# LayerNorm of x + residual: two loads moved ahead of the opening barrier, closing barriers dropped, wider x loads in a ring of 80 rows with a residual ring of 16

## Chip, cores, metric

One core of one Trainium2 chip. The metric is the device time of one execution in microseconds (us), of the slowest core (here the only one). "Span" is the time from the first to the last instruction that the profile records; the device time is 1.3 to 2.2 us longer, and that difference will matter. All timed runs that are compared here are fast, with a granted clock of 1.0.

The engines are named as in the profile: SP (SyncE) issues the large transfers, POOL (GpSimd), ACT (ScalarE) and DVE (VectorE) compute, PE (TensorE) does almost nothing here. SBUF and PSUM are the two memories on the chip.

## The reference

```python
# x, residual: (16, 1024, 512) float32; gamma, beta: (512,)
z = x + residual
mean = np.mean(z, axis=-1, keepdims=True)
var = np.var(z, axis=-1, keepdims=True)
return gamma * (z - mean) / np.sqrt(var + eps) + beta
```

That is 16384 rows of 512 numbers. The kernel puts 128 rows side by side in the 128 partitions, so it works on 128 "rows" per partition, and below a row always means one of these 128. One row of one tensor is 256 KB. x and residual are read and the result is written once: 100.7 MB in all.

## The kernel before

SP issues all large transfers on one queue, in program order. x is loaded into `zbuf` (a ring of 64 rows), residual into `rbuf` (a ring of 32). POOL adds residual to `zbuf`. ACT makes the mean and the sum of squares of each row. DVE normalizes in place, and SP stores from `zbuf`.

```python
X_CHUNKS = [8] * 15 + [4, 4]          # rows per load: 2 MB each, the last two 1 MB
R_CHUNKS = [8] * 15 + [4, 4]
OUT_CHUNKS = [16] * 7 + [8, 4, 4]     # 4 MB stores, the last three smaller
Z_ROWS = 64; R_ROWS = 32; STORE_LAG = 40; TURN = 8; JUNK = 4
...
    for c, (lo, n) in enumerate(loads_x):          # SP, in this order
        asked = lo + n
        while stored < asked - Z_ROWS:             # room in zbuf: an old store has landed
            ...; nc.sync.wait_ge(so[o], 16); ...
        nc.sync.dma_start(out=part(zbuf, Z_ROWS, lo, n), in_=dram(xf, lo, n)).then_inc(sx[c], 16)
        while todo_r and todo_r[0][1][0] + todo_r[0][1][1] <= asked:
            rc, (rlo, rn) = todo_r.pop(0)
            wait_rows(s_add, "add", rlo + rn - R_ROWS)   # room in rbuf: POOL has added
            nc.sync.dma_start(out=part(rbuf, R_ROWS, rlo, rn), ...).then_inc(sr[rc], 16)
        while todo_o and (olo + on <= asked - STORE_LAG or asked == total):  # (shortened)
            wait_rows(s_out, "out", olo + on)
            nc.sync.dma_start(out=dram(of, olo, on), in_=part(zbuf, ...)).then_inc(so[oc], 16)
...
    # ACT, in turns of 8 rows: every activation waits for the one 4 before it
    act.wait_ge(s_add, r0 + TURN)
    for k in range(2 * TURN):        # 8 Identity (mean), then 8 Square (variance)
        ...
        i.then_inc(s_act, 1).wait_op(s_act, due, "sem-ge")
    act.activation(out=std[...], in_=ssq[...], func=ACT.Sqrt, ...)
...
    # at the end: SP waits for the last stores, clears the semaphores;
    # leaving the tile context then adds drains and barriers of all engines
```

SP waits in order, so a wait of one transfer also holds back all later ones. And the load of residual rows that end at row r waits until POOL has added all rows up to r - R_ROWS.

Of the kernel before, what the change touches and what calls it, by code (L numbers as in the profile page):

```python
# [6 lines left out]

FP32 = mybir.dt.float32
ACT = mybir.ActivationFunctionType
ALU = mybir.AluOpType  # L10


X_CHUNKS = [8] * 15 + [4, 4]
R_CHUNKS = [8] * 15 + [4, 4]
OUT_CHUNKS = [16] * 7 + [8, 4, 4]

Z_ROWS = 64
R_ROWS = 32
STORE_LAG = 40


TURN = 8


JUNK = 4


@with_exitstack
def kernel(
# [9 lines left out]
    nc = tc.nc  # L39
    P = nc.NUM_PARTITIONS  # L40
    xf = x.flatten_outer_dims()
    rf = residual.flatten_outer_dims()
    of = out.flatten_outer_dims()
    N, D = xf.shape
    inv_d = 1.0 / float(D)
    total = N // P
    turns = total // TURN

    def spans(sizes):
        assert sum(sizes) == total  # L50
        return [(sum(sizes[:c]), n) for c, n in enumerate(sizes)]

    blocks = spans(OUT_CHUNKS)

    def dram(t, lo, n):

        b0, bn = next(b for b in blocks if b[0] <= lo and lo + n <= b[0] + b[1])
        v = t[P * b0 : P * (b0 + bn), :].rearrange("(p j) d -> p j d", p=P)
        return v[:, lo - b0 : lo - b0 + n, :].rearrange("p a b -> p (a b)")

    ctx.enter_context(tc.tile_critical())  # L61

    zbuf = nc.alloc_sbuf_tensor("zbuf", [P, Z_ROWS * D], FP32)
    rbuf = nc.alloc_sbuf_tensor("rbuf", [P, R_ROWS * D], FP32)
    gb_row = nc.alloc_sbuf_tensor("gb_row", [1, 2 * D], FP32)
# [3 lines left out]
    nm = nc.alloc_sbuf_tensor("nm", [P, total], FP32)  # L69
    ssq = nc.alloc_sbuf_tensor("ssq", [P, total], FP32)  # L70
# [1 line left out]
    rstd = nc.alloc_sbuf_tensor("rstd", [P, total], FP32)  # L72
    gamma_p = nc.alloc_psum_tensor("gamma_p", [P, D], FP32)
    beta_p = nc.alloc_psum_tensor("beta_p", [P, D], FP32)
    junk = [nc.alloc_psum_tensor(f"junk{i}", [P, D], FP32) for i in range(JUNK)]

    sems = []

    def sem(name):
        s = nc.alloc_semaphore(name)  # L80
        sems.append(s)
        return s

    loads_x, loads_r, stores = spans(X_CHUNKS), spans(R_CHUNKS), spans(OUT_CHUNKS)
    sx = [sem(f"sx{c}") for c in range(len(loads_x))]
    sr = [sem(f"sr{c}") for c in range(len(loads_r))]
    so = [sem(f"so{c}") for c in range(len(stores))]
    s_gb = [sem(f"gb{k}") for k in range(2)]
    s_const = sem("const")
    s_pe = sem("pe")  # L90
    s_add = sem("add")
    s_act = sem("act")
    s_std = sem("std")
    s_dve = sem("dve")
    s_out = sem("out")

    def part(buf, size, lo, n):
        assert lo % size + n <= size
        return buf[:, (lo % size) * D : (lo % size + n) * D]


    nc.scalar.dma_start(out=gb_row[:, :D], in_=gamma[None, :]).then_inc(s_gb[0], 16)
    nc.scalar.dma_start(out=gb_row[:, D:], in_=beta[None, :]).then_inc(s_gb[1], 16)
    nc.vector.memset(ones[:, :], 1.0).then_inc(s_const, 1)  # L104
    nc.vector.memset(eps_t[:, :], float(eps)).then_inc(s_const, 1)  # L105
    nc.tensor.wait_ge(s_const, 1)
# [6 lines left out]

    todo_r, todo_o = list(enumerate(loads_r)), list(enumerate(stores))
    seen = {"add": 0, "out": 0}

    def wait_rows(s, key, rows):
        if rows > seen[key]:
            nc.sync.wait_ge(s, rows)
            seen[key] = rows  # L120

    stored = 0
    for c, (lo, n) in enumerate(loads_x):
        asked = lo + n
        while stored < asked - Z_ROWS:
            o = next(i for i, b in enumerate(stores) if b[0] == stored)
            assert all(o != t[0] for t in todo_o)
            nc.sync.wait_ge(so[o], 16)
            stored += stores[o][1]
        nc.sync.dma_start(  # L130
            out=part(zbuf, Z_ROWS, lo, n), in_=dram(xf, lo, n)
        ).then_inc(sx[c], 16)
        while todo_r and todo_r[0][1][0] + todo_r[0][1][1] <= asked:
            rc, (rlo, rn) = todo_r.pop(0)
            wait_rows(s_add, "add", rlo + rn - R_ROWS)
            nc.sync.dma_start(  # L136
                out=part(rbuf, R_ROWS, rlo, rn), in_=dram(rf, rlo, rn)
            ).then_inc(sr[rc], 16)
        while todo_o and (
            todo_o[0][1][0] + todo_o[0][1][1] <= asked - STORE_LAG or asked == total  # L140
        ):
            oc, (olo, on) = todo_o.pop(0)
            wait_rows(s_out, "out", olo + on)
            nc.sync.dma_start(  # L144
                out=dram(of, olo, on), in_=part(zbuf, Z_ROWS, olo, on)
            ).then_inc(so[oc], 16)


    have_x = have_r = 0
    lo = 0  # L150
    while lo < total:
        n = min(loads_x[have_x][1], loads_r[have_r][1])
        nc.gpsimd.wait_ge(sx[have_x], 16)
        nc.gpsimd.wait_ge(sr[have_r], 16)
        assert loads_x[have_x] == loads_r[have_r] == (lo, n)
        z = part(zbuf, Z_ROWS, lo, n)
        nc.gpsimd.tensor_tensor(  # L157
            out=z, in0=z, in1=part(rbuf, R_ROWS, lo, n), op=ALU.add
        ).then_inc(s_add, n)
        have_x, have_r, lo = have_x + 1, have_r + 1, lo + n  # L160

    def row_at(zoff, k):
        return zbuf[:, bass.ds(zoff + k * D, D)]


    act = nc.scalar
    act.preload_act_table_set("sqrt_and_others")  # L167
    act.wait_ge(s_const, 2)
    act.sem_inc(s_act, JUNK)
    with act.Fori(0, turns) as t:  # L170
        zoff = act.snap((t * (TURN * D)) % (Z_ROWS * D))
        r0 = act.snap(t * TURN)

        n0 = act.snap(t * (2 * TURN))
        act.wait_ge(s_add, r0 + TURN)
        for k in range(2 * TURN):
            row = k % TURN


            due = act.lower_val(n0 + (k + 1))  # L180
            if k < TURN:
                i = act.activation(  # L182
                    out=junk[k % JUNK][:, :],
                    in_=row_at(zoff, row),
                    func=ACT.Identity,
                    scale=-inv_d,
                    accum_out=nm[:, bass.ds(r0 + row, 1)],
                )
            else:
                i = act.activation(  # L190
                    out=junk[k % JUNK][:, :],
                    in_=row_at(zoff, row),
                    func=ACT.Square,
                    bias=nm[:, bass.ds(r0 + row, 1)],
                    accum_out=ssq[:, bass.ds(r0 + row, 1)],
                )
            i.then_inc(s_act, 1).wait_op(s_act, due, "sem-ge")
        due = act.lower_val(n0 + (JUNK + 2 * TURN))
        act.activation(  # L199
            out=std[:, bass.ds(r0, TURN)],  # L200
            in_=ssq[:, bass.ds(r0, TURN)],
            func=ACT.Sqrt,
            bias=eps_t[:, 0:1],
            scale=inv_d,
        ).then_inc(s_std, TURN).wait_op(s_act, due, "sem-ge")


    dve = nc.vector
    dve.wait_ge(s_pe, 2)
    with dve.Fori(0, turns) as t:  # L210
        zoff = dve.snap((t * (TURN * D)) % (Z_ROWS * D))
        r0 = dve.snap(t * TURN)
        n0 = dve.snap(t * (2 * TURN))
        for k in range(TURN):
            due = dve.lower_val(n0 + (JUNK + TURN + k + 1))
            dve.scalar_tensor_tensor(  # L216
                out=row_at(zoff, k),
                in0=row_at(zoff, k),
                scalar=nm[:, bass.ds(r0 + k, 1)],
                in1=gamma_p[:, :],  # L220
                op0=ALU.add,
                op1=ALU.mult,
            ).wait_op(s_act, due, "sem-ge")
        due = dve.lower_val(r0 + TURN)
        dve.reciprocal(  # L225
            out=rstd[:, bass.ds(r0, TURN)], in_=std[:, bass.ds(r0, TURN)]
        ).then_inc(s_dve, TURN).wait_op(s_std, due, "sem-ge")
        for k in range(TURN):
            i = dve.scalar_tensor_tensor(  # L229
                out=row_at(zoff, k),  # L230
                in0=row_at(zoff, k),
                scalar=rstd[:, bass.ds(r0 + k, 1)],
                in1=beta_p[:, :],
                op0=ALU.mult,
                op1=ALU.add,
            )
            i.then_inc(s_out, 1)
            if k == 0:
                i.wait_op(s_dve, due, "sem-ge")


    for o, (lo, n) in enumerate(stores):
        if lo >= stored:
            nc.sync.wait_ge(so[o], 16)
    nums = sorted(s.num for s in sems)
    assert nums == list(range(nums[0], nums[-1] + 1)), nums
    nc.sync.sem_clear(range(nums[0], nums[-1] + 1))


# [33 lines left out]
```

## Time and profile before

| | before |
|---|---|
| time, median of 4 runs | 242.61 us (242.29 to 242.68) |
| span of the profiled run; its time | 240.0 us; 242.21 us |
| first load issued; first load landed | 0.94; 8.32 us |
| last store issued; landed | 231.14; 238.75 us |
| last landing to end of span | 1.28 us |

The landings are in the trace's semaphore records, which no view shown here prints: each transfer has 16 landing times there, one for each DMA engine, and a landing without further words is the last of them. The profile page says at once what the limit is; the digits are busy tenths in 40 slices of the span, 9 is 90% or more.

```profile
span 240.0 us, 1853 instructions
...
PE 4.1 (2%) x4; PEld 1.0 (0%) x4; DVE 178.7 (74%) x274; ACT 176.6 (74%) x529; POOL 142.2 (59%) x21
...
DVE  0000399999999999999997399944999359995950
ACT  2002999999999999999972999449993599959500
...
DMA  7999999999999999999999999999999999999994
GB/s 252 434 420 429 431 435 431 429 415 431 434 440 437 415 420 431 475 437 390 429 434 434 420 426 434 429 453 426 415 423 431 456 399 423 445 426 431 431 418 205
...
q1 hardware_dynamic: 6336, 100.67, 98.4%
```

DMA is at 9 in all slices but the first and last, at about 430 GB/s, and the queue's packets fill 98.4% of 16 engines' time. The Trainium skill ("DMA: Bandwidth & Descriptors", § Where 436 GB/s comes from) gives 435.2 GB/s as the ceiling of the SBUF ports; the trace agrees to 1%. ACT and DVE are at 9 in 26 of the 40 slices, yet they cost nothing while DMA is full.

SP's own timeline (start, duration, line, what) shows the opening: the first load goes out at 0.94 us, and eight more before any wait; the residual ring of 32 rows lets four residual loads go out at once.

```profile
0.94 0.39 SPq L130 DMA_DIRECT2D zbuf<-in_x_dram  x1
...
4.94 0.49 SPq L130 DMA_DIRECT2D zbuf<-in_x_dram  x1
22.17 0.33 SPq L136 DMA_DIRECT2D rbuf<-in_residual_dram  x1
```

How long that queue is can be read from the residual loads that went out between 40 and 90 us: the last line is the time from issue to landing.

```profile
L136 SPq DMA_DIRECT2D rbuf<-in_residual_dram x4: 328/379/431, 41.8 to 83.8; - x4
...
DMA to landing us min/median/max: 19.1/33.8/39.8
```

A residual load lands at least 19 us after its issue, although 2 MB take only 4.9 us to move. At least 14 us of other transfers stood before it. I call that time the lead.

The end, from the last store (issued at 231.1, landing 7.6 us later) and the barriers that follow:

```profile
L144 SPq DMA_DIRECT2D out_dram<-zbuf x1: 333/333/333, 231.1 to 231.1; - x1
...
DMA to landing us min/median/max: 7.6/7.6/7.6
```

```profile
L278 SPq EVENT_SEMAPHORE  x2: 17/17/17, 239.5 to 240.0; - x2
```

All five engines pass barriers until 240.0, after a last landing at 238.75.

The end of one of ACT's turns in the timeline:

```profile
32.28 0.67 ACT L190 ACTIVATE junk<-zbuf,nm 128x512 f32 x1
...
33.19 0.30 ACT L199 ACTIVATE std<-ssq,eps_t  x1
33.84 0.60 ACT L182 ACTIVATE junk<-zbuf 128x512 f32 x1 [0.35 <-issue]
```

The last Square starts at 32.28, the square root at 33.19 and the next turn at 33.84. A turn of 8 rows takes 11.41 us.

### The profile page before, as it was taken

Reading aid. Unit: us, or ns where it says so; the run is one execution under the profiler, and the core shown is the slowest. Engines: PE = TensorE matmul, PEld = TensorE weight load, DVE = VectorE, ACT = ScalarE, POOL = GpSimd, SP = SyncE. Lnnn points to the kernel's source line nnn. Section 1 sums busy time; section 2 is a strip of 40 time slices with the busy share of each in tenths; the row PEclk is TensorE's granted clock in tenths of the full one; section 3 lists DMA queues with packets and bytes.
Section 4 is the critical chain, followed back from the end, with each engine's and each line's share of the span. In section 5 each row is a group of like instructions: output and inputs, shape, how many; then the busy total and the mean of one; then the engine's idle time right before and its main releaser. Section 6 shows DMA issues by size and latency. Waiting matters only on the chain.

```text
span 240.0 us, 1853 instructions
## 1 busy us (share of the span) xinstructions
PE 4.1 (2%) x4; PEld 1.0 (0%) x4; DVE 178.7 (74%) x274; ACT 176.6 (74%) x529; POOL 142.2 (59%) x21
## 2 busy tenths in 40 slices
PE   3300000000000000000000000000000000000000
PEld 0000000000000000000000000000000000000000
DVE  0000399999999999999997399944999359995950
ACT  2002999999999999999972999449993599959500
POOL 0078989889899506894088920989109890860000
DMA  7999999999999999999999999999999999999994
GB/s 252 434 420 429 431 435 431 429 415 431 434 440 437 415 420 431 475 437 390 429 434 434 420 426 434 429 453 426 415 423 431 456 399 423 445 426 431 431 418 205
DMA packets 6341, 100.68 MB, mean 419 GB/s; under 512 B 706, under 2 KB 706, under 8 KB 708
## 3 DMA queue, kind: packets, MB, share of 16 engines
q1 hardware_dynamic: 6336, 100.67, 98.4%
q14 instruction: 1, 0.01, 0.0%
q10 hardware_dynamic: 4, 0.00, 0.0%
HBM read 67.11 MB, written 33.55 MB: 419 GB/s over the span
## 4 chain that ended last, share of the span: by engine, by line
DMA 56%; ACT 14%; issue 14%; POOL 6%; DVE 3%; SPq 2%; ACTq 2%; DVEq 0%; POOLq 0%
DMA out_dram<-zbuf 36%; DMA rbuf<-in_residual_dram 20%; ACT junk L190 9%; POOL zbuf L157 6%; ACT junk L182 5%; DVE zbuf L229 3%; SPq L130 1%; ACTq L180 1%; ACTq L182 1%; SPq L136 1%; ACT std L199 0%; SPq L144 0%; DVE rstd L225 0%; DVEq L229 0%; ACTq L170 0%
## 5 line engine op out<-in xcount | busy, mean ns | idle before, releaser
L157 POOL TENSOR_TENSOR zbuf<-zbuf,rbuf 128x4096 f32<-128x4096 f32 (+1 forms) x17 | 142.0, 8351 | 71.5 <-DMA rbuf<-in_residual_dram 71.5
L216 DVE SCALAR_TENSOR_TENSOR zbuf<-zbuf,nm,gamma_p 128x512 f32 x128 | 91.0, 747 | 50.8 <-ACT junk L190 50.8
L182 ACT ACTIVATE junk<-zbuf 128x512 f32 x128 | 74.4, 581 | 45.3 <-POOL zbuf L157 41.6
L229 DVE SCALAR_TENSOR_TENSOR zbuf<-zbuf,rstd,beta_p 128x512 f32 x128 | 85.7, 743 | 0.6
L190 ACT ACTIVATE junk<-zbuf,nm 128x512 f32 x128 | 86.1, 673 | 0.0
L190 ACT ACTIVATION_READ_ACCUMULATOR junk<-zbuf,nm x128 | 24.2, 189 | 0.0
L182 ACT ACTIVATION_READ_ACCUMULATOR junk<-zbuf x128 | 23.9, 187 | 0.0
L199 ACT ACTIVATE std<-ssq,eps_t x16 | 4.8, 301 | 1.6
L225 DVE RECIPROCAL rstd<-std x16 | 3.1, 196 | 0.0
L167 ACT ACT_TABLE_LOAD x1 | 1.3, 1283 | 1.7 <-SPq L61 1.7
L109 PE MATMUL beta_p<-gb_row,ones 1*128 1x512 f32 x2 | 2.1, 1136 | 2.4 <-DMA gb_row<-in_beta_dram 2.4
L109 PE MATMUL gamma_p<-gb_row,ones 1*128 1x512 f32 x2 | 2.0, 1122 | 2.3 <-DMA gb_row<-in_gamma_dram 2.3
L104 DVE MEMSET ones<- 1x128 f32 x1 | 0.2, 165 | 1.0 <-SPq L61 1.0
L109 PEld LDWEIGHTS beta_p<-gb_row,ones 1*128 1x128 f32 x2 | 0.5, 304 | 4.0 <-DMA gb_row<-in_beta_dram 4.0
L109 PEld LDWEIGHTS gamma_p<-gb_row,ones 1*128 1x128 f32 x2 | 0.5, 305 | 2.3 <-issue 2.3
L264 POOL MEMSET const-float32-0.0<- 128x1 f32 x1 | 0.1, 99 | 0.2 <-issue 0.2
L264 POOL MEMSET const-bfloat16-1.0<- 128x1 bf16 x1 | 0.1, 102 | 0.0
L264 POOL MEMSET const-uint8-127<- 128x1 uint8 x1 | 0.1, 102 | 0.0
L264 POOL MEMSET const-float32-1.0<- 128x1 f32 x1 | 0.1, 99 | 0.0
L105 DVE MEMSET eps_t<- 128x1 f32 x1 | 0.1, 59 | 0.0
## 6 DMA issues: line engine op xcount, KB each, us to landing
zbuf<-in_x_dram SPq DMA_DIRECT2D x15, 2048.0 KB, 32.8
rbuf<-in_residual_dram SPq DMA_DIRECT2D x15, 2048.0 KB, 30.4
out_dram<-zbuf SPq DMA_DIRECT2D x7, 4096.0 KB, 28.5
zbuf<-in_x_dram SPq DMA_DIRECT2D x2, 1024.0 KB, 32.6
rbuf<-in_residual_dram SPq DMA_DIRECT2D x2, 1024.0 KB, 34.6
out_dram<-zbuf SPq DMA_DIRECT2D x1, 2048.0 KB, 16.5
out_dram<-zbuf SPq DMA_DIRECT2D x2, 1024.0 KB, 7.7
gb_row<-in_gamma_dram ACTq DMA_DIRECT2D x1, 2.0 KB
```

The lines of the kernel that those rows point to most:

```text
L109: nc.tensor.matmul(dest[:, :], ones[:, :], gb_row[:, k * D : (k + 1) * D], start=True, stop=True).then_inc(s_pe, 1)
L130: nc.sync.dma_start(out=part(zbuf, Z_ROWS, lo, n), in_=dram(xf, lo, n)).then_inc(sx[c], 16)
L136: nc.sync.dma_start(out=part(rbuf, R_ROWS, rlo, rn), in_=dram(rf, rlo, rn)).then_inc(sr[rc], 16)
L157: nc.gpsimd.tensor_tensor(out=z, in0=z, in1=part(rbuf, R_ROWS, lo, n), op=ALU.add).then_inc(s_add, n)
L167: act.preload_act_table_set("sqrt_and_others")
L180: due = act.lower_val(n0 + (k + 1))
L182: i = act.activation(out=junk[k % JUNK][:, :], in_=row_at(zoff, row), func=ACT.Identity, scale=-inv_d, accum_out=nm[:, bass.ds(r0 + row, 1)],)
L190: i = act.activation(out=junk[k % JUNK][:, :], in_=row_at(zoff, row), func=ACT.Square, bias=nm[:, bass.ds(r0 + row, 1)], accum_out=ssq[:, ...
L199: act.activation(out=std[:, bass.ds(r0, TURN)], in_=ssq[:, bass.ds(r0, TURN)], func=ACT.Sqrt, bias=eps_t[:, 0:1], scale=inv_d,).then_inc(s ...
L216: dve.scalar_tensor_tensor(out=row_at(zoff, k), in0=row_at(zoff, k), scalar=nm[:, bass.ds(r0 + k, 1)], in1=gamma_p[:, :], op0=ALU.add, op1 ...
L225: dve.reciprocal(out=rstd[:, bass.ds(r0, TURN)], in_=std[:, bass.ds(r0, TURN)]).then_inc(s_dve, TURN).wait_op(s_std, due, "sem-ge")
L229: i = dve.scalar_tensor_tensor(out=row_at(zoff, k), in0=row_at(zoff, k), scalar=rstd[:, bass.ds(r0 + k, 1)], in1=beta_p[:, :], op0=ALU.mul ...
```

## The change

It sets out to start the stream earlier, to end it without barriers, and to move x in fewer and larger transfers. The 4 MB loads of x come with a larger `zbuf` ring (80 rows); the memory for that comes from the residual ring (16 rows instead of 32). ACT and DVE work in turns of 4 rows with plain waits between the passes: the engine waits until its own earlier instructions are done, which the texts below call a drain. Core of the diff (cut):

```diff
-X_CHUNKS = [8] * 15 + [4, 4]
+X_CHUNKS = [8] * 2 + [16] * 6 + [8, 4, 4]
-Z_ROWS = 64
-R_ROWS = 32
+Z_ROWS = 80
+R_ROWS = 16
-TURN = 8
-JUNK = 4
+ADD = 8
+TURN = 4
+EARLY = 2
...
+    tc.close()            # the scheduler's closing steps come here, ahead of the work
+    tc.compile()
-    ctx.enter_context(tc.tile_critical())
...
+    junk_m = [... 4 tensors in PSUM]
+    junk_s = [... 2 tensors in PSUM, 2 in SBUF]
...
+    for o, (lo, n) in enumerate(stores[:-1]):
+        if lo >= stored:
+            nc.sync.wait_ge(so[o], 16)
+    nc.sync.sem_clear(range(nums[0], nums[-1]))      # while the last store moves
+    nc.sync.wait_ge(so[-1], 16)
+    nc.sync.sem_clear(range(nums[-1], nums[-1] + 1))
...
     # ACT, DVE: per-instruction waits gone, one wait between passes
+        act.wait_ge(s_act, r0 * 2 + TURN)
...
+    # the first EARLY transfers go to the front of the first block, before its Drain
+    at = next(n for n, i in enumerate(opening) if i.opcode == "Drain")
+    blks[0].instructions = opening[:at] + first + opening[at:]
```

POOL's adds stay at 8 rows each. The order on SP's queue becomes: x (16 rows), residual (8), residual (8), store (16), and so on.

More of the change, by code (lines that the diff above doesn't have):

```diff
@@ L6 @@
 from concourse._compat import with_exitstack
+from concourse.ordered_engine_set import OrderedEngineSet
 FP32 = mybir.dt.float32
@@ L74 @@
     beta_p = nc.alloc_psum_tensor("beta_p", [P, D], FP32)
-    junk = [nc.alloc_psum_tensor(f"junk{i}", [P, D], FP32) for i in range(JUNK)]
+    junk_m = [nc.alloc_psum_tensor(f"junk_m{i}", [P, D], FP32) for i in range(TURN)]
+    junk_s = [nc.alloc_psum_tensor(f"junk_s{i}", [P, D], FP32) for i in range(6 - TURN)]
+    junk_s += [
+        nc.alloc_sbuf_tensor(f"junk_s{i}", [P, D], FP32) for i in range(6 - TURN, TURN)
+    ]
     sems = []
@@ L82, in sem @@
         return s
-    loads_x, loads_r, stores = spans(X_CHUNKS), spans(R_CHUNKS), spans(OUT_CHUNKS)
+    loads_x, loads_r, stores = spans(X_CHUNKS), spans(R_CHUNKS), blocks
     sx = [sem(f"sx{c}") for c in range(len(loads_x))]
     sr = [sem(f"sr{c}") for c in range(len(loads_r))]
-    so = [sem(f"so{c}") for c in range(len(stores))]
     s_gb = [sem(f"gb{k}") for k in range(2)]
@@ L95 @@
     s_out = sem("out")
+    so = [sem(f"so{c}") for c in range(len(stores))]
+    nums = [s.num for s in sems]
+    assert nums == list(range(nums[0], nums[-1] + 1)), nums
     def part(buf, size, lo, n):
@@ L99, in part @@
         return buf[:, (lo % size) * D : (lo % size + n) * D]
-    nc.scalar.dma_start(out=gb_row[:, :D], in_=gamma[None, :]).then_inc(s_gb[0], 16)
-    nc.scalar.dma_start(out=gb_row[:, D:], in_=beta[None, :]).then_inc(s_gb[1], 16)
+    for k, src in enumerate((gamma, beta)):
+        nc.scalar.dma_start(out=gb_row[:, k * D : (k + 1) * D], in_=src[None, :]).then_inc(
+            s_gb[k], 16
+        )
     nc.vector.memset(ones[:, :], 1.0).then_inc(s_const, 1)
@@ L115 @@
     seen = {"add": 0, "out": 0}
+    first = []
     def wait_rows(s, key, rows):
@@ L120, in wait_rows, with move @@
             seen[key] = rows
+    def move(out, in_, s):
+        i = nc.sync.dma_start(out=out, in_=in_).then_inc(s, 16)
+        if len(first) < EARLY:
+            first.append(i.ins)
     stored = 0
@@ L129 @@
             stored += stores[o][1]
-        nc.sync.dma_start(
-            out=part(zbuf, Z_ROWS, lo, n), in_=dram(xf, lo, n)
-        ).then_inc(sx[c], 16)
+        move(part(zbuf, Z_ROWS, lo, n), dram(xf, lo, n), sx[c])
         while todo_r and todo_r[0][1][0] + todo_r[0][1][1] <= asked:
@@ L135 @@
             wait_rows(s_add, "add", rlo + rn - R_ROWS)
-            nc.sync.dma_start(
-                out=part(rbuf, R_ROWS, rlo, rn), in_=dram(rf, rlo, rn)
-            ).then_inc(sr[rc], 16)
+            move(part(rbuf, R_ROWS, rlo, rn), dram(rf, rlo, rn), sr[rc])
         while todo_o and (
@@ L143 @@
             wait_rows(s_out, "out", olo + on)
-            nc.sync.dma_start(
-                out=dram(of, olo, on), in_=part(zbuf, Z_ROWS, olo, on)
-            ).then_inc(so[oc], 16)
-    have_x = have_r = 0
-    lo = 0
-    while lo < total:
-        n = min(loads_x[have_x][1], loads_r[have_r][1])
-        nc.gpsimd.wait_ge(sx[have_x], 16)
-        nc.gpsimd.wait_ge(sr[have_r], 16)
-        assert loads_x[have_x] == loads_r[have_r] == (lo, n)
-        z = part(zbuf, Z_ROWS, lo, n)
-        nc.gpsimd.tensor_tensor(
-            out=z, in0=z, in1=part(rbuf, R_ROWS, lo, n), op=ALU.add
-        ).then_inc(s_add, n)
-        have_x, have_r, lo = have_x + 1, have_r + 1, lo + n
-    def row_at(zoff, k):
-        return zbuf[:, bass.ds(zoff + k * D, D)]
+            move(dram(of, olo, on), part(zbuf, Z_ROWS, olo, on), so[oc])
+    for o, (lo, n) in enumerate(stores[:-1]):
[4 more added lines that the diff above has]
+    nc.sync.sem_clear(range(nums[-1], nums[-1] + 1))
+    for c, (lo, n) in enumerate(loads_x):
+        nc.gpsimd.wait_ge(sx[c], 16)
+        for rc, (rlo, rn) in enumerate(loads_r):
+            if lo <= rlo < lo + n:
+                assert rlo + rn <= lo + n
+                nc.gpsimd.wait_ge(sr[rc], 16)
+                for a in range(rlo, rlo + rn, ADD):
+                    an = min(ADD, rlo + rn - a)
+                    z = part(zbuf, Z_ROWS, a, an)
+                    nc.gpsimd.tensor_tensor(
+                        out=z, in0=z, in1=part(rbuf, R_ROWS, a, an), op=ALU.add
+                    ).then_inc(s_add, an)
     act = nc.scalar
@@ L168 @@
     act.wait_ge(s_const, 2)
-    act.sem_inc(s_act, JUNK)
     with act.Fori(0, turns) as t:
@@ L172 @@
         r0 = act.snap(t * TURN)
-        n0 = act.snap(t * (2 * TURN))
         act.wait_ge(s_add, r0 + TURN)
-        for k in range(2 * TURN):
-            row = k % TURN
-            due = act.lower_val(n0 + (k + 1))
-            if k < TURN:
-                i = act.activation(
-                    out=junk[k % JUNK][:, :],
-                    in_=row_at(zoff, row),
-                    func=ACT.Identity,
-                    scale=-inv_d,
-                    accum_out=nm[:, bass.ds(r0 + row, 1)],
-                )
-            else:
-                i = act.activation(
-                    out=junk[k % JUNK][:, :],
-                    in_=row_at(zoff, row),
-                    func=ACT.Square,
-                    bias=nm[:, bass.ds(r0 + row, 1)],
-                    accum_out=ssq[:, bass.ds(r0 + row, 1)],
-                )
-            i.then_inc(s_act, 1).wait_op(s_act, due, "sem-ge")
-        due = act.lower_val(n0 + (JUNK + 2 * TURN))
+        for k in range(TURN):
+            act.activation(
+                out=junk_m[k][:, :],
+                in_=zbuf[:, bass.ds(zoff + k * D, D)],
+                func=ACT.Identity,
+                scale=-inv_d,
+                accum_out=nm[:, bass.ds(r0 + k, 1)],
+            ).then_inc(s_act, 1)
+        act.wait_ge(s_act, r0 * 2 + TURN)
+        for k in range(TURN):
+            act.activation(
+                out=junk_s[k][:, :],
+                in_=zbuf[:, bass.ds(zoff + k * D, D)],
+                func=ACT.Square,
+                bias=nm[:, bass.ds(r0 + k, 1)],
+                accum_out=ssq[:, bass.ds(r0 + k, 1)],
+            ).then_inc(s_act, 1)
+        act.wait_ge(s_act, r0 * 2 + 2 * TURN)
         act.activation(
@@ L204 @@
             scale=inv_d,
-        ).then_inc(s_std, TURN).wait_op(s_act, due, "sem-ge")
+        ).then_inc(s_std, TURN)
     dve = nc.vector
@@ L212 @@
         r0 = dve.snap(t * TURN)
-        n0 = dve.snap(t * (2 * TURN))
+        dve.wait_ge(s_act, r0 * 2 + 2 * TURN)
         for k in range(TURN):
-            due = dve.lower_val(n0 + (JUNK + TURN + k + 1))
+            row = zbuf[:, bass.ds(zoff + k * D, D)]
             dve.scalar_tensor_tensor(
-                out=row_at(zoff, k),
-                in0=row_at(zoff, k),
+                out=row,
+                in0=row,
                 scalar=nm[:, bass.ds(r0 + k, 1)],
@@ L222 @@
                 op1=ALU.mult,
-            ).wait_op(s_act, due, "sem-ge")
-        due = dve.lower_val(r0 + TURN)
+            )
+        dve.wait_ge(s_std, r0 + TURN)
         dve.reciprocal(
             out=rstd[:, bass.ds(r0, TURN)], in_=std[:, bass.ds(r0, TURN)]
-        ).then_inc(s_dve, TURN).wait_op(s_std, due, "sem-ge")
+        ).then_inc(s_dve, TURN)
+        dve.wait_ge(s_dve, r0 + TURN)
         for k in range(TURN):
-            i = dve.scalar_tensor_tensor(
-                out=row_at(zoff, k),
-                in0=row_at(zoff, k),
+            row = zbuf[:, bass.ds(zoff + k * D, D)]
+            dve.scalar_tensor_tensor(
+                out=row,
+                in0=row,
                 scalar=rstd[:, bass.ds(r0 + k, 1)],
@@ L235 @@
                 op1=ALU.add,
-            )
-            i.then_inc(s_out, 1)
-            if k == 0:
-                i.wait_op(s_dve, due, "sem-ge")
-    for o, (lo, n) in enumerate(stores):
-        if lo >= stored:
-            nc.sync.wait_ge(so[o], 16)
-    nums = sorted(s.num for s in sems)
-    assert nums == list(range(nums[0], nums[-1] + 1)), nums
-    nc.sync.sem_clear(range(nums[0], nums[-1] + 1))
+            ).then_inc(s_out, 1)
+    blks = nc.main_func.blocks
+    names = {i.name for i in first}
+    for b in blks[1:]:
+        kept = [i for i in b.instructions if i.name not in names]
+        if len(kept) < len(b.instructions):
+            b.instructions = kept
+    opening = list(blks[0].instructions)
+    at = next(n for n, i in enumerate(opening) if i.opcode == "Drain")
+    blks[0].instructions = opening[:at] + first + opening[at:]
 _INS = ['x', 'residual', 'gamma', 'beta', 'eps']
```

## The prediction

> **What bounds the kernel now.** DMA. The page's third part puts 98.4% of 16 engines' span on the one load/store queue; in the 40-slice view every slice but the first and the last is at 9. The packet records show all 16 engines full from about 2.0 to 236.7 us, at 430 GB/s on average, with no hole. The Trainium skill ("DMA: Bandwidth & Descriptors", § Where 436 GB/s comes from) gives 435.2 GB/s as ceiling; the trace agrees to about 1%. DVE and ACT (74% busy each) cost nothing while the queue stays full. Only the edges are left: the first load is issued at 0.94 us, after the opening barrier; the last store lands at 238.75 us, the span ends at 240.03.
>
> **What the change does, costed.**
> 1. First two loads ahead of the barrier: first issue near 0 instead of 0.94 us: about -0.9 us, all on the path, as the queue never rests afterwards.
> 2. No closing barriers: before, 1.28 us pass from the last landing to the end (semaphore clear, two rounds of drains). Left over: one wait and a clear, about 0.2 us. About -1.1 us.
> 3. x in 4 MB loads: 32 KB packets take 1.213 us, two 16 KB packets 1.224 us. 48 such pairs per engine: about -0.5 us.
> 4. Residual ring of 16 rows: load k+2 now waits for add k. An add of 8 rows takes 8.88 us, plus 0.2 us of handing over; 8 rows of x and residual take 9.8 us of DMA. Carrying landings and adds forward with these durations, the queue is ahead by 3 to 10 us until the load of rows 40-48 at about 55 us, where issue comes about as the queue runs out. I put +0.6 us there (0 to 1.5). From the first store on, slack is about 10 us.
> 5. ACT in turns of 4 rows instead of 8, with two drains in each. Now: 11.41 us for 8 rows: spacing 0.613 us (Identity), 0.705 us (Square), 0.87 us of turn overhead. (The skill, "ScalarE: Activation LUTs", § What ACT_TABLE_LOAD costs, says a [128,1] pointer operand adds about 93 ns; the trace shows 92.) After: 1.85 + 0.88 + 2.12 + 0.97 + 0.6 = about 6.4 to 6.5 us for 4 rows, so 12.9 for 8. ACT, now busy without a break, takes 32 x 6.45 = 206 us from 21.5 us on; DVE then needs about 5.7 us after the last squares, so the last store is issued near 233 us. The DMA-bound end needs it by about 233. So ACT becomes nearly co-critical: each 0.1 us more per turn would cost 3 us. I allow +0.3 us and a long upper tail.
>
> Sum: 242.6 - 0.9 - 1.1 - 0.5 + 0.6 + 0.3 = 241.0 us; range 239.6 to 244.0. Faster by over 2%: 3%; within 2%: 91%; slower by over 2%: 6%.
>
> **What would show it.** First load at the span's start; end of span about 0.2 us after the last landing; 4 MB x loads landing in about 9.7 us steps; POOL's adds back to back before 60 us, a DMA dip, if any, near 55 us; ACT turn near 6.45 us, ACT over 85% busy, DVE waiting for ACT; last store issued near 233 us, against 231.1 now.
>
> **What would make it wrong.** An ACT turn of 6.7 us or more (slower drains, or writing two of the four junk outputs to SBUF): the last store then comes late and the time passes 246. A larger dip near 55 us, or several. Or the 2 us of launch outside the span moving with the barriers.

## More of the kernel before

The waits of SP's queue (line, for whom, us in total, times, longest) show that it spends most of the time waiting for room, with a long queue in front of it:

```profile
SPq L130 <- DMA out_dram<-zbuf: 110.9, 4, 29.7
SPq L144 <- DVE zbuf L229: 65.5, 7, 29.1
SPq L136 <- POOL zbuf L157: 35.0, 4, 16.7
```

## The result

| | before | after |
|---|---|---|
| time, median of 4 runs each | 242.61 us | 240.87 us (240.75 to 241.11) |
| span and time of the profiled run | 240.0; 242.21 us | 239.8; 241.11 us |
| first load issued; landed | 0.94; 8.32 us | 0.00; 7.23 us |
| last store issued; landed | 231.14; 238.75 us | 229.58; 239.74 us |
| first to last landing | 230.43 us | 232.51 us |
| last landing to end of span | 1.28 us | 0.05 us |
| time minus span | 2.18 us | 1.31 us |

The ratio of after to before is 0.993 (95% interval 0.992 to 0.995). Ratios here are the mean time of one kernel's fast runs over that of the other's of the same rounds, so not quite the ratio of the medians in the tables. It is clear of noise, but under the 2% that would count as faster.

The time fell by less than 1%, nearly what was predicted. But look at the fifth row: the stretch between the two edges became 2.1 us longer. The page of after:

```profile
span 239.8 us, 1798 instructions
...
PE 3.7 (2%) x4; PEld 1.2 (0%) x4; DVE 177.3 (74%) x290; ACT 186.6 (78%) x545; POOL 142.0 (59%) x21
...
DMA  8999989999999999999999999999999999999995
GB/s 315 432 435 481 437 380 435 432 418 380 470 391 418 355 437 432 432 429 451 437 437 407 426 462 437 421 410 429 445 418 424 443 432 405 459 432 437 404 420 247
```

The first slice rose from 252 to 315 GB/s: the early start. The tenth (54 to 60 us) fell from 431 to 380 and the fourteenth (78 to 84 us) from 415 to 355. These two only say where to look: the view counts a packet whole in the slice in which it starts, so a change of packet size shows as well. The sixth slice also reads 380, though nothing was lost there. The opening on SP's timeline:

```profile
0.00 0.39 SPq L138 DMA_DIRECT2D zbuf<-in_x_dram  x1
0.44 0.43 SPq L138 DMA_DIRECT2D rbuf<-in_residual_dram  x1
1.92 0.33 SPq L138 DMA_DIRECT2D zbuf<-in_x_dram  x1
...
21.11 10.16 SPq L138 DMA_DIRECT2D rbuf<-in_residual_dram  x2
```

The two early loads are there, at 0.00 and 0.44. Of the residual only two loads go out before the first wait at 21.11 (before: four), because the ring now holds two.

The waits of SP turned around: they are no longer waits for stores, but for POOL's adds.

```profile
SPq L138 <- POOL zbuf L181: 169.1, 14, 20.1
SPq L138 <- DVE zbuf L243: 44.7, 7, 19.6
```

The chain of waits that ended last, in order of time, shows the loop that this makes in the first 60 us: residual load, add, residual load, add.

```profile
12.28 8.81 POOL zbuf L181
...
21.11 15.41 DMA rbuf<-in_residual_dram
...
36.68 8.90 POOL zbuf L181
...
45.59 10.43 DMA rbuf<-in_residual_dram
```

A residual load is issued at the very moment an add ends (21.11, 45.59), and an add starts when a load has landed (36.68). Time from issue to landing (min, median, max) of the residual loads that went out between 40 and 90 us:

```profile
DMA to landing us min/median/max: 7.4/10.4/21.2
```

The shortest time from issue to landing fell from 19.1 to 7.4 us. That load (issued at 54.42, rows 40 to 48) took about as long as the first load of all (7.23 us), which had nothing ahead of it: it went out only 1.6 us before the transfer ahead of it landed. Stretches of the trace from A to B us (busy us and instructions of PE, PEld, DVE, ACT, POOL; then clock, DMA share, GB/s), first before, then after:

```profile
core 0: us, PE busy (x) PEld busy (x) DVE busy (x) ACT busy (x) POOL busy (x), PEclk, DMA share, GB/s
...
54.00:57.00 3.00, 0.00 (x0) 0.00 (x0) 2.96 (x6) 2.57 (x8) 3.00 (x1) 1.00 1.01 431
```

```profile
54.00:57.00 3.00, 0.00 (x0) 0.00 (x0) 2.96 (x7) 2.88 (x9) 1.21 (x2) 1.00 0.98 339
```

339 GB/s against 431 in these 3 us (all packets in them are of 16 KB). In the packet records the engines pause there one after another, between 55.2 and 55.9 us (at the lowest point 9 of 16 have a packet under way), and the next packet takes 0.9 to 1.55 us on 14 of them instead of 0.61. A second loss does not show as a pause: the load of rows 56 to 64, issued at 73.91, 2.5 us before the transfer ahead of it landed, took 8.5 us to land,

```profile
L138 SPq DMA_DIRECT2D rbuf<-in_residual_dram x1: 328/328/328, 73.9 to 73.9; - x1
...
DMA to landing us min/median/max: 8.5/8.5/8.5
```

and 43 packets between 78 and 82 us, two or three an engine on average, took 0.75 to 1.3 us (0.61 is usual). I call the time from one landing to the next a step. A residual load usually has a step of 4.89 us; these two had 5.77 and 5.99 us: 0.9 and 1.1 us lost. (By the mean of the 16 landing times it is 0.7 and 1.1 us; the rest of the first is one engine falling behind.)

The end of after:

```profile
L138 SPq DMA_DIRECT2D out_dram<-zbuf x1: 332/332/332, 229.6 to 229.6; - x1
...
DMA to landing us min/median/max: 10.2/10.2/10.2
```

```profile
L169 SPq EVENT_SEMAPHORE_RANGE_CLEAR  x1: 39/39/39, 239.8 to 239.8; - x1
```

The last store now stands 10.2 us in the queue, so ACT and DVE were in time. After it lands, one clear of 39 ns is all that is left. One of ACT's turns of 4 rows (Identity at 33.71 and on, Square at 36.39 and on, square root at 39.44, next turn at 39.92):

```profile
33.71 0.60 ACT L194 ACTIVATE junk_m<-zbuf 128x512 f32 x1 [0.18 <-issue]
...
36.09 0.19 ACT L194 ACTIVATION_READ_ACCUMULATOR junk_m<-zbuf  x1
36.39 0.69 ACT L203 ACTIVATE junk_s<-zbuf,nm 128x512 f32 x1
...
39.44 0.30 ACT L211 ACTIVATE std<-ssq,eps_t  x1
39.92 0.60 ACT L194 ACTIVATE junk_m<-zbuf 128x512 f32 x1 [0.18 <-issue]
```

From 33.71 to 39.92 is 6.21 us for 4 rows; I had predicted 6.45.

### The profile page after: what moved, and what is told of

Its sections match the earlier page's. It is cut to its first block, busy times and chain, and to the rows that moved or that the text cites. A ratio compares the mean times of both kernels' runs of the same rounds, so it can differ in the third digit from the quotient of the medians.

```text
span 239.8 us, 1798 instructions
## 1 busy us (share of the span) xinstructions
PE 3.7 (2%) x4; PEld 1.2 (0%) x4; DVE 177.3 (74%) x290; ACT 186.6 (78%) x545; POOL 142.0 (59%) x21
## 4 chain that ended last, share of the span: by engine, by line
DMA 53%; POOL 30%; ACT 8%; issue 3%; DVE 2%; ACTq 1%; DVEq 0%; SPq 0%; POOLq 0%
DMA rbuf<-in_residual_dram 53%; POOL zbuf L181 30%; ACT junk_s L203 4%; ACT junk_m L194 4%; DVE zbuf L228 1%; DVE zbuf L243 1%; ACTq L194 0%; ACTq L203 0%; SPq L138 0%; POOLq L177 0%; DVEq L228 0%; ACTq L189 0%; ACTq L201 0%; ACT std L211 0%; ACTq L210 0%
## 5 line engine op out<-in xcount | busy, mean ns | idle before, releaser
L228 DVE SCALAR_TENSOR_TENSOR zbuf<-zbuf,nm,gamma_p 128x512 f32 x128 | 87.1, 743 | 49.2 <-ACT junk_s L203 49.2
L194 ACT ACTIVATE junk_m<-zbuf 128x512 f32 x128 | 74.9, 585 | 27.3 <-POOL zbuf L181 22.1
L203 ACT ACTIVATE junk_s<-zbuf,nm 128x512 f32 x128 | 88.8, 694 | 3.9
L243 DVE SCALAR_TENSOR_TENSOR zbuf<-zbuf,rstd,beta_p 128x512 f32 x128 | 87.1, 744 | 1.1
L194 ACT ACTIVATION_READ_ACCUMULATOR junk_m<-zbuf x128 | 23.9, 187 | 0.0
L203 ACT ACTIVATION_READ_ACCUMULATOR junk_s<-zbuf,nm x128 | 23.9, 187 | 0.0
L211 ACT ACTIVATE std<-ssq,eps_t x32 | 9.5, 297 | 3.7
L237 DVE RECIPROCAL rstd<-std x32 | 5.5, 171 | 0.0
```

Source lines behind the costliest of these rows:

```text
L194: act.activation(out=junk_m[k][:, :], in_=zbuf[:, bass.ds(zoff + k * D, D)], func=ACT.Identity, scale=-inv_d, accum_out=nm[:, bass.ds(r0 + ...
L203: act.activation(out=junk_s[k][:, :], in_=zbuf[:, bass.ds(zoff + k * D, D)], func=ACT.Square, bias=nm[:, bass.ds(r0 + k, 1)], accum_out=ss ...
L211: act.activation(out=std[:, bass.ds(r0, TURN)], in_=ssq[:, bass.ds(r0, TURN)], func=ACT.Sqrt, bias=eps_t[:, 0:1], scale=inv_d,).then_inc(s ...
L228: dve.scalar_tensor_tensor(out=row, in0=row, scalar=nm[:, bass.ds(r0 + k, 1)], in1=gamma_p[:, :], op0=ALU.add, op1=ALU.mult,)
L237: dve.reciprocal(out=rstd[:, bass.ds(r0, TURN)], in_=std[:, bass.ds(r0, TURN)]).then_inc(s_dve, TURN)
L243: dve.scalar_tensor_tensor(out=row, in0=row, scalar=rstd[:, bass.ds(r0 + k, 1)], in1=beta_p[:, :], op0=ALU.mult, op1=ALU.add,).then_inc(s_ ...
```

## The experiments

Ten kernels, all correct. Each is the kernel after with one edit, but e7, which is the kernel before with one edit. Times are medians; "before" is the kernel before, on the same chip in the same rounds.

| run | time us | before us | ratio (95%) | first to last landing us | time minus span us |
|---|---|---|---|---|---|
| e0 after again | 241.28 | 242.38 | 0.994 (0.993 to 0.996) | 232.70 | 1.30 to 1.35 |
| e1 no early loads | 242.54 | 242.38 | 1.000 (0.998 to 1.001) | 232.46 | 1.29 to 1.36 |
| e2 closing barriers back | 242.22 | 242.38 | 0.998 (0.997 to 1.000) | 232.63 | 1.73 to 1.84 |
| e3 x in 2 MB loads | 239.81 | 242.71 | 0.987 (0.986 to 0.989) | 231.10 | 1.31 to 1.34 |
| e4 rings and loads of before | 239.56 | 242.38 | 0.988 (0.986 to 0.990) | 230.57 | 1.35 to 1.37 |
| e5 2 MB loads to row 48, then 4 MB | 240.20 | 242.71 | 0.989 (0.987 to 0.990) | 231.52 | 1.28 to 1.34 |
| e6 turns of 2 rows (one run) | 257.67 | 242.71 | | 248.89 | 1.27 |
| e7 before, with rings and loads of after | 245.12 | 242.71 | 1.008 (1.006 to 1.011) | 233.56 | 2.13 to 2.21 |
| e8 residual in 1 MB loads | 240.30 | 242.33 | 0.991 (0.990 to 0.992) | 231.76 | 1.28 to 1.34 |
| e9 rows 48 to 64 of x in two loads (one run) | 242.00 | 242.33 | | 233.33 | 1.30 |

The kernel before had a time minus span of 2.13 to 2.23 us in all of its runs here.

### e0_after: does the trace repeat?

No edit.

> The changed kernel once more, to see whether its trace repeats. The page of after shows two losses in the middle: the load of residual rows 40-48 lands 5.77 us after the transfer before it (4.89 us is usual), and the load of rows 56-64 5.99 us after (packets slow from 78.6 to 82 us). Theory: the first is the residual ring's (16 rows) and repeats within 0.2 us; the second, if the ring causes it, repeats too. Rival: the second is chance of that one execution, then that step is 4.9 to 5.0 us here and the span is 1.1 us shorter, 238.7. Time 240.6 to 241.1, ratio to before 0.992 to 0.994.

The two steps took 5.76 and 6.03 us, as in the first trace, and the slow packets lie at the same place. So both belong to the kernel; the rival for the second falls. The time was 0.2 us above the range that I gave, the ratio just above its edge.

### e1_early0: no loads ahead of the barrier

```diff
-EARLY = 2
+EARLY = 0
```

> After, with no load ahead of the opening barrier. Theory: the whole stream of transfers shifts by the later first issue (0.95 us instead of 0), so time is 0.9 to 1.1 us above after (241.8), span about 240.7, time minus span of the profiled run stays at 1.3 us. Rival: the time outside the span (2.2 us before, 1.3 us after) shrank because the opening moved; then time minus span goes back to 2.2 us here and time is nearer 242.7.

The loss was larger than expected: 242.54 against 241.28, so 1.26 us. The trace says why: the first issue comes at 1.39 us, not at 0.95. The new layout has three rounds of the opening barrier where before had one and a step of its own, as the scheduler's closing steps now stand ahead of the work. Time minus span stayed at 1.3, so what shrank outside the span has nothing to do with the early loads.

### e2_close: two barriers of all engines put back at the end

```diff
+    nc.all_engine_barrier()
+    nc.all_engine_barrier()
     blks = nc.main_func.blocks
```

> After, with two barriers of all engines put back at the end. Theory: without them the engines that are done early go through the launch's own closing steps while the last stores still move, and so the time outside the span fell by 0.9 us as well. Then here the span ends about 0.7 to 1.2 us after the last landing (after: 0.05), time minus span goes back to 2.0 to 2.2 us, time is 1.5 to 2.0 us above after, 242.4 to 242.9. Rival: the part outside the span has nothing to do with closing barriers; then time rises by 0.7 to 1.2 us only and time minus span stays at 1.3 us.

The span now ended 0.64 us after the last landing (0.05 without), and time minus span rose from 1.3 to 1.73 to 1.84 us. So closing barriers cost twice: in the span, and outside it, where nothing in the profile shows it. The rival, that it stays at 1.3, falls. But the part outside came back only by half: 0.5 of 0.9 us. The time rose by 0.94 us, less than the 1.5 that I expected. The rest of the difference outside the span belongs to something else in which before and after differ (at the end of before, for one, POOL clears semaphores once more); what it is, no run here tells. That engines which are done early go through the launch's own closing steps meanwhile is my explanation, not shown: these steps leave no record in the trace. The Trainium skill ("Runtime: NRT & Kernel Launch", § The ~15µs preamble/postamble breakdown) does list a barrier and semaphore resets after the kernel among the launch's stages; no run here shows their length.

### e4_ring64: rings and loads of before under the new edges

```diff
-X_CHUNKS = [8] * 2 + [16] * 6 + [8, 4, 4]
+X_CHUNKS = [8] * 15 + [4, 4]
-Z_ROWS = 80
-R_ROWS = 16
+Z_ROWS = 64
+R_ROWS = 32
```

> After with the rings of before (64 and 32 rows) and x in 2 MB loads; edges, engine code and barriers as in after. Theory: the ring of 16 rows with 4 MB loads costs about 2 us in the middle and the 32 KB packets of x give back only 0.4. So here no step of a residual load is over 5.0 us, first to last landing takes 230.3 to 230.7 us (before 230.4, after 232.5), time is 1.2 to 2.0 us under after: 239.0 to 239.7, ratio 0.985 to 0.988. Rival: the longer middle comes from the engines (turns of 4 rows, drains) or from stores and loads mixing; then it stays at 232 us or more.

All as expected: no residual step over 4.92 us, 230.57 us from first to last landing, 239.56 us. This kernel has the turns of 4 rows and the early start, so the rival that puts the longer middle down to them falls. The edges, with the turns of 4 rows, are worth 2.8 us; the rings and the 4 MB loads gave back over half of it.

### e7_before_rings: the other half

```diff
 # the kernel before
-X_CHUNKS = [8] * 15 + [4, 4]
+X_CHUNKS = [8] * 2 + [16] * 6 + [8, 4, 4]
-Z_ROWS = 64
-R_ROWS = 32
+Z_ROWS = 80
+R_ROWS = 16
 # and POOL's loop waits for x and residual loads of different size, as in after
```

> Before (its edges, its engine code in turns of 8 rows, its closing) with only the rings of 80 and 16 rows and the 4 MB loads of x. Theory: the load order costs the same 2 us here as in after, since POOL's adds set it and they are the same: residual rows 40-48 land 5.4 to 6 us after the transfer before, first to last landing 232.3 to 232.9 us (before 230.4), time 244.2 to 245.0, ratio 1.007 to 1.011: slower than before. Rival: the longer middle in after comes from the turns of 4 rows or from the early start; then this kernel stays at 230.5 us and takes 242.2 to 242.7.

Slower than before by 2.4 us, with steps of 5.63 us (rows 40 to 48) and 6.12 us (rows 56 to 64), at the same places as in after. The rings with their loads lose time at the same places in both shells. First to last landing came out at 233.56 us, 0.7 above my range, and the time 0.1 above. One DMA engine lagged more than usual (see the last section), and that cost twice: it ended 2.4 us after the mean of the 16 (1.9 in after); and at rows 16 to 24 it was already 0.6 us late (the last engine in after: 0.15), so POOL's adds, which wait for the last engine, and the residual loads behind them came later, and the step of rows 40 to 48 lost 1.1 us by the mean (0.7 in after).

### e3_x8: is it the small ring, or the load order?

```diff
-X_CHUNKS = [8] * 2 + [16] * 6 + [8, 4, 4]
+X_CHUNKS = [8] * 15 + [4, 4]
```

> After with all of x in 2 MB loads, rings of 80 and 16 rows kept. Theory (lead, not ring): no residual step over 5.1 us before 100 us, first to last landing 230.3 to 230.8 us, time 239.4 to 239.8, so the same as with rings of 64 and 32 rows (239.56) within 0.2 us, and about 0.3 us slower than the mixed loads, which have four times 128 packets of 32 KB more. Rival (the small ring costs by itself): 232 us or more, time over 240.8.

239.81 us, with the ring of 16 rows kept. No residual step was over 4.9 us. The residual loads between 40 and 90 us went from issue to landing in

```profile
DMA to landing us min/median/max: 10.5/10.5/20.3
```

against 7.4, 10.4 and 21.2 in after. So the small ring does not cost by itself. The ring and the 4 MB loads together do, by the order in which they let SP issue. First to last landing (231.10) was 0.3 us above my range, again by the one lagging engine.

### e5_mix6: 2 MB loads only while the lead is short

```diff
-X_CHUNKS = [8] * 2 + [16] * 6 + [8, 4, 4]
+X_CHUNKS = [8] * 6 + [16] * 4 + [8, 4, 4]
```

> After with the first 48 rows of x in six 2 MB loads, then four 4 MB loads; rings of 80 and 16 rows kept. Theory: what costs is that two residual loads are issued just as the queue runs out: a 4 MB load of x and two residual loads per step leave the second residual load with no lead (issue to landing 7.4 and 8.5 us in after, where 10 us or more is safe). With 2 MB loads each residual load goes out some 10.4 us before it lands, so neither the step at 55 us nor the slow packets near 80 us come back: no residual step over 5.1 us before 100 us, first to last landing 230.1 to 230.6 us, time 239.1 to 239.6, ratio 0.985 to 0.988, a shade faster than the version with the rings of before. Rival: the 16-row ring costs by itself, whatever the load order; then first to last landing stays over 232 us. Second rival, for the slow packets alone: they come with the first store after a residual load; then they are here too.

No pause, no slow packets, no residual step over 4.91 us before 100 us, although the first store again follows the load of rows 56 to 64 directly: the second rival falls. But the time of 240.20 us missed my range; the version is not faster than e3 or e4. First to last landing, 231.52 us, missed its range too. The 16 landing times of the last store are at 236.4 us in the mean, as in e4 (236.5), but the last one is 2.4 us later, in e4 1.5 us. That engine takes more than the larger packets saved.

### e9_late8: moving the loss on purpose

```diff
-X_CHUNKS = [8] * 2 + [16] * 6 + [8, 4, 4]
+X_CHUNKS = [8, 8, 16, 16, 8, 8, 16, 16, 16, 8, 4, 4]
```

> After with the loads of rows 48-64 of x in two of 2 MB, all others as in after. Carried forward with the durations of the trace, the residual load of rows 40-48 still has no lead (step 5.5 to 5.9 us, as in after), that of rows 48-56, which had 4 us of lead in after, now has none (step 5.5 to 6.3 us; 4.9 in after), and that of rows 56-64, which lost 1.1 us in after, comes with lead (step under 5.1 us). Rival: the slow packets near 80 us belong to those rows or to the first store's start, not to the lead; then rows 56-64 stay slow or nothing is slow at rows 48-56.

This was the sharpest test: the edit gives lead to one load and takes it from another. Rows 40 to 48 took 5.86 us, as in after. Rows 48 to 56, harmless in after (4.91 us), now took 7.43 us, even more than expected. Rows 56 to 64 went back to 4.90 us. SP's timeline shows the load of rows 48 to 56 going out at 65.10, 1.7 us before the transfer ahead of it landed, and the table of stretches the drop around it, at 64 to 72 us:

```profile
65.10 0.33 SPq L138 DMA_DIRECT2D rbuf<-in_residual_dram  x1
```

```profile
54.00:57.00 3.00, 0.00 (x0) 0.00 (x0) 2.96 (x7) 2.88 (x9) 1.21 (x2) 1.00 0.95 333
...
64.00:68.00 4.00, 0.00 (x0) 0.00 (x0) 3.58 (x7) 3.58 (x12) 4.00 (x2) 1.00 0.94 336
68.00:72.00 4.00, 0.00 (x0) 0.00 (x0) 3.36 (x6) 3.71 (x12) 4.00 (x1) 1.00 1.04 328
72.00:78.00 6.00, 0.00 (x0) 0.00 (x0) 5.33 (x9) 5.58 (x18) 5.54 (x2) 1.00 1.02 431
```

Lost rate follows lost lead, not the rows: that it belongs to rows 56 to 64 falls. The first store is another matter. It moved as well, and in e9 it stands right behind rows 48 to 56, so this run alone does not clear it; e5 does, where the first store stands behind a load with lead and nothing is slow, and so do rows 40 to 48, which are slow with no store behind them. How large a loss is, lead alone does not tell: issued 1.6 to 2.5 us before the landing ahead, a load lost 0.9 us with a load of x behind it, and 1.1 and 2.5 us with a store behind it. Whether a store adds to the loss, no run here tells.

### e8_r4: the residual ring in quarters

```diff
-R_CHUNKS = [8] * 15 + [4, 4]
+R_CHUNKS = [8] * 2 + [4] * 28
```

> After with residual loads of 4 rows (1 MB) from row 16 on; rings of 80 and 16 rows and the 4 MB loads of x kept. Theory: the loss comes from giving the residual ring back in halves; in quarters a load waits for an add that ended one 4-row add earlier, carrying landings and adds forward no load finds the queue empty. So no slow packets near 80 us and no hole near 55 us, mean packet time of the 16 engines 0.8 to 1.2 us below after in spite of 8 KB packets; last landing 238.0 to 239.2[...], time 239.4 to 240.4. Rival: a ring of 16 rows with 4 MB loads costs 2 us however it is cut; then time is 240.8 or more.

POOL's adds become 4 rows long with the loads. No pause and no slow packets between 50 and 90 us, with the 4 MB loads and the ring of 16 rows kept; 240.30 us, so the rival falls. One number missed: the packet time summed over one engine is 236.7 us in the mean, as in after, not 0.8 to 1.2 us below. The 8 KB packets took 0.313 us in the mean, 1.5% more per byte than the 16 KB ones of before (0.617), and that took away most of what the slow packets had cost. The 16 landing times of the last store still came at 237.2 us in the mean, against 237.8 in after.

### e6_turn2: where ACT would become the limit

```diff
-TURN = 4
+TURN = 2
```

> After in turns of 2 rows. A turn of 4 took ACT 6.21 us, of which 4 x (0.613 + 0.705) is rows and 0.93 us is waits, square root and loop. Theory: the 0.93 us is per turn, so a turn of 2 takes 3.57 us, ACT ends near 250 us instead of 222, the last store is issued at about 250 to 253 us into an empty queue and lands about 5 us later; time 254 to 259, ratio 1.05 to 1.07; ACT over 85% busy. It shows where the limit on ACT's turn lies that the prediction feared and that after stays clear of. Rival: turns cost little because ACT waits for data anyway; time under 244.

257.67 us, as worked out from 0.93 us of waits, square root and loop per turn. ACT was busy for 79% of the span only, not over 85%: the waits inside a turn do not count as busy. From the page:

```profile
span 256.4 us, 2182 instructions
...
PE 3.7 (1%) x4; PEld 1.2 (0%) x4; DVE 184.9 (72%) x322; ACT 202.9 (79%) x577; POOL 141.8 (55%) x21
...
DMA  8999999999999999999999999999999999095733
```

The queue runs dry near the end (the 0 and the 5733). The last store, into an empty queue, shows what a 1 MB store takes without a queue, from issue to landing:

```profile
DMA to landing us min/median/max: 3.9/3.9/3.9
```

In after the last store landed 10.2 us after its issue, so it stood 6.3 us behind others. Divided by 32 turns, ACT's turn could have been at least about 0.2 us longer before it cost anything. That is an estimate; ACT also waited once for POOL in after, for 4.3 us, which would have taken up a part.

## Why the prediction came out right

The time was predicted to 0.1 us, but that is partly luck: the terms were off in both directions. The measured column takes the profiled pair, whose times differ by 1.10 us (the medians by 1.74: of before a fast execution was profiled, of after the slowest of four; the table does not explain that spread). For the transfers it takes the mean of the 16 landing times, so that the slowest engine has a row of its own.

| term | predicted us | measured us | from |
|---|---|---|---|
| earlier start | -0.9 | -1.0 | mean first landing 8.07 to 7.09; e1 |
| closing, inside the span | -1.1 | -1.2 | 1.28 to 0.05; e2 |
| closing, outside the span | 0 | -0.9 | 2.18 to 1.31; e2 shows half of it |
| larger packets of x | -0.5 | -0.4 | 48 x (2 x 0.611 - 1.213) |
| residual ring | +0.6 | +1.8 | mean steps of 5.56 and 6.01 against 4.89; e4, e7, e9 |
| ACT in turns of 4 | +0.3 | 0 | last store 6.3 us in the queue |
| slowest DMA engine | not seen | +0.6 | 1.3 us behind the mean before, 1.9 after |
| sum | -1.6 | -1.1 | times of the profiled pair: -1.1 |

1. **DMA is the limit, only edges count: right.** e4, which changes the edges (and the turns) and leaves rings and loads, gains 2.8 us.
2. **The start: right**, and on the path in full.
3. **The closing: right inside the span, mis-sized in all.** "Left over: one wait and a clear, about 0.2 us" came out at 0.05. That 0.9 us outside the span would go as well stood only among the things that would make the prediction wrong.
4. **Packets of 32 KB: right**, 0.4 us.
5. **The residual ring: right mechanism, mis-sized term.** The prediction put the hole near 55 us, where it is, at "+0.6 us there (0 to 1.5)"; by the mean of the engines it cost 0.7. It then said that slack returns with the first store, and that is so. But the load just ahead of that store, rows 56 to 64 at 74 us, has hardly any lead either and lost 1.1 us, and the prediction has no term for it. It looked for a place where the queue runs out; here the queue did not run out (no pause in the packets), and the load ran slowly all the same.
6. **ACT: mis-sized.** A turn took 6.21, not 6.45 us: the two stretches with a drain took 0.84 and 0.93 us, not 0.88 and 0.97, and the loop's end 0.48, not 0.6 us. ACT was busy 78%, not over 85%, and the last store went out at 229.6, not 233. The fear behind the long upper tail was sound (e6), but after stays clear of it.

What was not foreseen at all is that the end is set by the slowest of 16 engines. The ring and the slowest engine cost 1.8 us more than predicted; the part outside the span took back 0.9 and ACT 0.3. That the errors cancelled is no merit of the method.

The Trainium skill ("ScalarE: Activation LUTs", § ACT is a hardware spline evaluator) says that ACT writes faster to PSUM than to SBUF. I had feared that for the two junk outputs in SBUF. In after's trace Squares into SBUF have records of 0.707 us, into PSUM 0.67 to 0.69; but they start 0.705 us apart (0.721 after the first, which goes to PSUM), so writing to SBUF lost nothing.

The best versions measured are e4 (239.56 us, ratio 0.988) and e3 (239.81 us, ratio 0.987): the new edges with 2 MB loads. Both beat before and after; they can't be told apart.

## What to carry to other kernels

When DMA is full, as here, ask of every transfer how much other work stands before it in the queue at its issue; the time from issue to landing, minus the transfer's own time, shows it. A ring that is given back in halves and a queue that waits in order can use up that lead though the bytes and the engines' times are unchanged, and larger transfers make the order coarser. Count the edges too: two barriers at the end cost 0.6 us in the span and 0.5 us outside it (e2), so look at time minus span as well as at the span.

## What the Trainium skill lacked or had wrong

- "DMA: Bandwidth & Descriptors" has a fixed cost of about 2 us per transfer (§ Anatomy of one DMA, fitted on the other issue path); the first 2 MB load in after landed after 7.23 us where 4.89 us is the step in a full queue, so 2.3 us: this agrees. It lacks what follows: 2 MB loads issued 10.4 us or more ahead of their landing lost nothing (e3, e5), while those at 7.4 and 8.5 us in after lost 0.9 and 1.1 us, and one at 9.1 us in e9 lost 2.5. Put as issue before the landing of the transfer ahead: 5.5 us or more was harmless, 2.5 us or less was not, and what lies between was not measured.
- The same page calls two of the engines usually slower and, as its best guess, ties that to the other issue path. Here all large transfers are issued from SP, and in every run one landing time of the 16 fell behind: at the last store it came 1.3 us after their mean in before and 1.5 to 2.4 us in the others, while the second latest was mostly 0.2 to 0.6 us behind. (Only in e6, where the queue ran dry, had it caught up at the end, to 0.1 us.) The lag grows in small jumps, mostly at stores. The packed trace does not name the engine, and the cause is open.
- The same page lacks packet times for large rows: 0.309 us for 8 KB, 0.611 for 16 KB, 1.213 for 32 KB (medians in after; 0.312 for the 8 KB of e8, most of them loads), so per byte 1.1% less from the first to the second and 0.7% less from the second to the third.
- "Runtime: NRT & Kernel Launch" gives the launch a length of its own. The runs show that what the kernel does at its end changes what comes after it: time minus span 2.2 us with the closing of before, 1.8 with two barriers, 1.3 with none.
